# Experts' weights fetched in rows of 8 KB a partition instead of 4 KB

## The chip, the cores and the metric

One NeuronCore of a Trainium2 chip runs the kernel alone. The metric is device time in microseconds for one launch, and the kernel before took 886.41 us (median of 3 runs, 886.3 to 887.85). The engines are TensorE (PE, with its weight loads as PEld), VectorE (DVE), ScalarE (ACT), GpSimd (POOL) and SyncE (SP), which here only issues DMAs. Sixteen DMA engines move data between HBM and SBUF.

## The reference

The kernel computes one decoder layer for 512 tokens of width 1024 in float32: a combined projection, an HGRN2 branch and a stick-breaking attention branch, a mix with LayerNorm, a cross attention with LayerNorm, and a mixture of experts with a last LayerNorm. The change touches the weights of the last part:

```
for e in range(N_EXPERTS):                     # 16 experts, each token uses two of them
    hidden = jax.nn.silu(hf @ w1[e]) * (hf @ w3[e])    # w1[e], w3[e]: 1024 x 512
    y = y + combine[:, e:e + 1] * (hidden @ w2[e])     # w2[e]: 512 x 1024
```

Every expert reads 6.3 MB of weights, 2.1 MB for each matrix, and all sixteen are read whole.

## The kernel before

The program runs in the order of the layer. All weights come through one list: the class Weights keeps the sources in the order of use (`src`), a list of free buffers (`raw_free`), and issues one DMA from SP (line 54) as soon as a buffer comes free. A buffer holds 128 partitions x 4 KB, 512 KB in all. The dense part (everything up to the cross attention) splits each piece into two float32r parts on ACT and DVE (lines 65 and 67) and gives the buffer back at once. The experts' pieces are "plain": PE reads them as they land, and the buffer is given back by `done` when the expert is through. Towards the experts more and more SBUF becomes buffers (`ring`, `xres`, `s8`, `out` slots, parts of `sbk` and `wx`), until 44 of 512 KB are in use, three and a half experts' weights.

From expert 1 on a piece of w1 or w3 is two neighbouring rows of the matrix in each partition, 4 KB in a row; a piece of w2 is one row of 1024 numbers in each partition, 4 KB too. An expert has 12 pieces: four each of w1, w3 and w2. Expert 0 takes its rows 128 apart, 2 KB each.

The loop over the experts, in the order in which each engine meets it:

1. `up(e)`: PE multiplies the gathered tokens (64 columns) by w1 and w3 (line 1451); for more than 64 and 96 tokens two further parts follow under a branch (line 1462). ACT and DVE make the hidden values (lines 1472, 1473).
2. `turn_in(e + 1)`: eight transposes on PE (line 1424) of the next expert's tokens, which an indirect DMA of POOL has gathered (`gather`, line 1187). Then POOL issues the gather after that.
3. `down(e - 1)`: PE multiplies the hidden values of the expert before by its w2 (line 1492, further parts in line 1500) into `sums_down`.
4. `to_rows(e - 1)`: ACT (lines 1515, 1521) and then DVE (line 1523) scale the sums into the one tile `y_out`, and POOL adds its rows to the DRAM tensor `yd` by an indirect DMA (`scatter`, line 1301). `y_out` exists once, so `to_rows` of the next expert waits until this scatter has landed.
5. `turn_hidden(e)`: four transposes (line 1479), copied to SBUF on DVE (line 1481). DVE works in program order, so this copy stands behind `to_rows(e - 1)`, and `down(e)` needs it.

Steps 4, 5 and 3 make a ring: scatter lands, `to_rows` runs, the next scatter is issued, and so on; the copy behind `to_rows` holds the next `down` on PE. After the loop the last two experts are added without a scatter, and the last LayerNorm follows.

Of the kernel before, what the change touches and what calls it, by code (L numbers as in the profile page):

```python
# [24 lines left out]
class Weights:  # L25


    def __init__(self, nc, ahead):
        self.nc, self.ahead = nc, ahead
        self.other = ()  # L30
        self.src, self.raw_free, self.raw, self.parts = [], [], {}, {}
        self.out_free, self.own = [], {}
        self.kept = None
        self.plain = set()
        self.loaded = self.split = 0
        self.limit = 1 << 30

    def add(self, ap, plain=False):
# [5 lines left out]
        return j  # L44

    def buffers(self, raw=(), out=()):
        self.raw_free += raw
        self.out_free += out
        self.load()

    def load(self):
        while self.raw_free and self.loaded < len(self.src):
            ap, buf = self.src[self.loaded], self.raw_free.pop(0)
            self.nc.sync.dma_start(buf.rearrange("p (k n) -> p k n", n=ap.shape[-1]), ap)
            self.raw[self.loaded] = buf
            self.loaded += 1

    def prepare(self, upto):
        while self.split <= min(upto, self.limit, len(self.src) - 1):
            j = self.split  # L60
            if not self.out_free:
                return
            hi, lo = self.own[j] = self.out_free.pop(0)
            raw = self.raw.pop(j)
            self.nc.scalar.copy(hi, raw)  # L65
            eng = self.nc.gpsimd if j in self.other else self.nc.vector
            eng.tensor_tensor(lo, raw, hi.bitcast(F32), op=ALU.subtract)  # L67
            n = self.src[j].shape[-1]
            self.parts[j] = tuple(a.rearrange("p (k n) -> p k n", n=n) for a in (hi, lo))
            self.split += 1  # L70
            self.raw_free.append(raw)
            self.load()

    def get(self, j):
        if j in self.plain:
            return self.raw[j]
        self.prepare(j + self.ahead)
        return self.parts[j]

    def done(self, j):  # L80
        if j in self.plain:
            self.raw_free.append(self.raw.pop(j))
# [14 lines left out]
def tile_kernel(ctx, tc, x, mem, ln_in_g, ln_in_b, w_in, hg_lb_logits, hg_norm_g, w_branch_a, w_branch_b,  # L97
# [74 lines left out]
    outs = [out_tile(i) for i in range(4)]  # L172
    W.buffers([raws[:, i] for i in range(2)], outs)
    nc.sync.dma_start(xres[:, 1], x[P:2 * P])
    W.buffers([raws[:, i] for i in (2, 3)])
    for t in (2, 3):
# [270 lines left out]
    G = slot(10, [P, NT, 512], name="hgG")  # L447
    wx = pp.tile([P, 2, T], F32, name="wx")
    sbk = pp.tile([P, 2, T + 1], F32, name="sbk")
    oTa_h = oTa_l = None  # L450
# [261 lines left out]
    W.kept = None  # L712
    W.buffers([sbk.rearrange("p a n -> p (a n)")[:, 0:D]], [out_tile(3)])
    xres = pp.tile([P, NT, D], F32, tag="xres", name="xres1")
# [175 lines left out]
    def ring(tags):  # L890
        for i in tags:
            r = slot(i, [P, 2, D], name=f"ring{i}")
            rings[i] = [r[:, 0], r[:, 1]]
            W.buffers(rings[i])

# [79 lines left out]
    s8 = slot(8, [P, 2, D], name="s8")  # L975
    W.buffers([s8[:, 1], wx.rearrange("p a n -> p (a n)")])
    room = [s8[:, 0], rw.rearrange("p k n -> p (k n)")]
# [253 lines left out]
    more = take([10], I32, where=1)  # L1231

    natural_major([q_wo[1]], oc(0), oc(1), ev_wo, before=lambda t: begin(route_first(t), 2))
    for i in range(4):
        r = pp.tile([P, 2, D], F32, tag=f"out{i}", name=f"ringout{i}")
        W.buffers([r[:, 0], r[:, 1]])
    gather0(1, 0)
# [7 lines left out]
    route_fold(t)  # L1245
    W.buffers([xres[:, 0]])
    gather0(2, 0)
# [7 lines left out]
    gather0(3, 1)  # L1255
    s3 = slot(3, [P, 2, D], name="s3")
    W.buffers([s3[:, 1]])
    xgT = s3[:, 0].rearrange("p (k n) -> p k n", n=P)
# [3 lines left out]
    W.buffers([xres[:, 1]])  # L1262

# [126 lines left out]
    def tell():  # L1390
# [4 lines left out]
        yield 1  # L1395
        W.buffers([xres[:, 2], xres[:, 3]])
        count_blocks()
# [21 lines left out]
    def turn_in(e):  # L1419
        xg = gbr[:, 1].rearrange("t (q p k) -> t q k p", q=4, k=2)  # L1420
        for q in range(2):
            p = msp()
            for i in range(4):
                nc.tensor.transpose(p[:, i * P:(i + 1) * P], xg[:, 2 * q + i // 2, i % 2], ident)  # L1424
            (nc.scalar.copy, nc.vector.tensor_copy)[q](xgT[:, 4 * q:4 * q + 4],
# [17 lines left out]
    def up(e):  # L1443
        x, (a, b) = xgT, sums_up
        ws = []
        for q, js in enumerate(q_up[e]):
            ws.append([W.get(j) for j in js])
            for k in range(2):
                c = 2 * q + k
                for i, w in enumerate(reversed(ws[q])):  # L1450
                    nc.tensor.matmul(a[64 * i:64 * i + 64], x[:, c, 0:64], w[:, k * 512:(k + 1) * 512], start=c == 0,  # L1451
                                     stop=c == 7)
            tick()
        if e == 0:
# [3 lines left out]
        def part(g):  # L1458
            for c in range(8):
                for i in range(4):  # L1460
                    o = c % 2 * 512 + i % 2 * 256
                    nc.tensor.matmul(b[32 * i:32 * i + 32, 256 * g:256 * g + 256],  # L1462
                                     x[:, c, 64 + 32 * g:96 + 32 * g], ws[c // 2][i // 2][:, o:o + 256],
                                     start=c == 0, stop=c == 7)
# [10 lines left out]

    def turn_hidden(e, h, p=None):
        p = p or msp()
# [6 lines left out]
    def down(e):  # L1484

        x, (a, b) = hT.pop(e), sums_down
        ws = [W.get(j) for j in q_w2[e]]

        def base():
            for k, w in enumerate(ws):  # L1490
                for n in range(2):
                    nc.tensor.matmul(a[64 * n:64 * n + 64], x[:, k, 0:64], w[:, n * 512:(n + 1) * 512], start=k == 0,
                                     stop=k == 3)
                tick()

        def part(g):
            for k, w in enumerate(ws):
                s = slice(64 + 32 * (k // 2), 96 + 32 * (k // 2))
                for i in range(4):
                    nc.tensor.matmul(b[32 * i:32 * i + 32, 256 * g:256 * g + 256], x[:, 2 * g + k % 2, s],  # L1500
                                     w[:, 256 * i:256 * i + 256], start=k == 0, stop=k == 3)

# [23 lines left out]
    for e in range(NE - 1):  # L1526
# [4 lines left out]
        if e == 13:  # L1531
            scratch.extend(W.raw_free.pop() for i in range(4))
            more_blocks()
            W.buffers(scratch)
        if e == 0:
# [16 lines left out]
    def last_loads():  # L1552

        assert W.loaded == len(W.src)
        whole = [i for i in rings if all(any(b is f for f in W.raw_free) for b in rings[i])][:4]
        free.extend(b for b in W.raw_free if b is not s3[:, 1] and not any(b is h for i in whole for h in rings[i]))
        for t in (1, 2, 3, 0):
# [48 lines left out]
    yh[NE - 2], yl[NE - 2] = two_parts(rooms.pop(), "yg14")  # L1606
    yh[NE - 1], yl[NE - 1] = two_parts(3, "yg15")
    base, rest = down(NE - 2)
    base()

    p = msp()
    for i in range(4):
        nc.tensor.transpose(p[:, i * P:(i + 1) * P], h[:, i * P:(i + 1) * P], ident)
    x = work("w2k", [P, T], bufs=5).rearrange("p (k n) -> p k n", n=P)
# [5 lines left out]
    rest()  # L1620
    ws = [W.get(j) for j in q_w2[NE - 1]]
    for n in range(2):
        for k, w in enumerate(ws):
            nc.tensor.matmul(sums_up[n], x[:, k], w[:, halves[n]], start=k == 0, stop=k == 3)  # L1624
    for j in q_w2[NE - 1]:
# [95 lines left out]
```

## Time and profile before

| | us |
|---|---|
| median of 3 runs | 886.41 |
| profiled execution, its own time | 886.88 |
| span in the profile (first to last instruction) | 885.1 |
| PE busy | 847.2 (96%) |
| experts, from the first `up` to the last | 594.9 to 842 |

The page shows PE busy nearly throughout; the ends of matmuls are modelled there, so that a busy PE need not be one at its peak, and small gaps have to be looked for in the waits and the timeline. The DMA engines are nearly idle in the first two thirds and over 90% busy while the experts run, at some 350 to 390 GB/s.

### The profile page before, as it was taken

To read this page: it belongs to the slowest core of one execution; us is meant where nothing else is said; L and a number is where in the kernel's file an instruction comes from. 1 tells how busy PE (TensorE), PEld (TensorE's weight loads), DVE (VectorE), ACT (ScalarE), POOL (GpSimd) and SP (SyncE) were. 2 spreads that over 40 slices of the span, in tenths; PEclk is the share of its full clock that TensorE was granted. 3 is DMA by queue.
4 is the path that set the end of the run, shared out by engine and by line. 5 is a ranking of instruction groups with operands and counts; after the bars stand their busy time and mean duration, and the time that the engine had idled before them with its cause. 6 is when DMAs were issued, how large, how long until landed. Compare 5 with 4: busy or idle time off the path is not lost. (4 is left out here: it accounts for less than half of the span.)

```text
span 885.1 us, 13705 instructions
## 1 busy us (share of the span) xinstructions
PE 847.2 (96%) x5296; PEld 586.1 (66%) x5296; DVE 457.1 (52%) x806; ACT 337.7 (38%) x640; POOL 123.8 (14%) x212
## 2 busy tenths in 40 slices
PE   6999999999999999999999999997989999999994
PEld 5888777788777777888988888773333343344343
DVE  6632578644558554759744566684242322422336
ACT  2332336543554553422633444222332333323234
POOL 5400000000212220002200000221121111211102
PEclk8999999999999999999999999999999999999998
DMA  8443222222212227332742567599999999999952
GB/s 299 140 135 96 73 93 76 72 72 72 95 48 72 72 78 256 119 118 73 219 167 70 187 220 284 215 351 373 392 378 364 346 350 351 359 360 357 361 172 95
DMA packets 63908, 177.66 MB, mean 201 GB/s; under 512 B 7797, under 2 KB 7829, under 8 KB 63824
## 3 DMA queue, kind: packets, MB, share of 16 engines
q1 hardware_dynamic: 56144, 157.31, 49.6%
q0 software_dynamic: 7536, 18.65, 6.9%
q8 instruction: 60, 0.98, 0.4%
q10 hardware_dynamic: 144, 0.52, 0.1%
q14 instruction: 24, 0.20, 0.1%
HBM read 168.47 MB, written 15.73 MB: 208 GB/s over the span
## 5 line engine op out<-in xcount | busy, mean ns | idle before, releaser
L1523 DVE TENSOR_SCALAR ringgb<-I-5383_acc,wgb 32x256 f32<-32x256 f32 x60 | 29.2, 487 | 118.2 <-ACT ringgb L1521 116.7
L1451 PE MATMUL I-5377_acc<-ring,s 128*64 128x512 f32 x276 | 79.0, 596 | 0.0
L1515 ACT ACTIVATE ringgb<-I-5381_acc,wgb 64x512 f32<-64x512 f32 x30 | 20.5, 684 | 80.8 <-DMA yd<-ringgb,s 64.9
L67 DVE TENSOR_TENSOR I-69_out<-raws,I-69_out 128x1024 fp32r<-128x1024 f32 x24 | 29.4, 1224 | 38.3 <-ACT I-69_out L65 37.9
L1451 PEld LDWEIGHTS I-5377_acc<-ring,s 128*64 128x64 f32 x276 | 23.7, 137 | 34.0 <-issue 31.5
L1301 POOL DMA_INDIRECT yd<-ringgb,s x14 | 22.4, 1600 | 157.1 <-DVE I-8384w2k L1481 16.9
L663 DVE TENSOR_TENSOR_SCAN wx<-sbk 128x128 f32<-128x128 f32 (+3 forms) x32 | 27.1, 847 | 28.7 <-POOL sbk L659 28.7
L65 ACT CAST I-73_out<-raws 128x1024 fp32r<-128x1024 f32 x23 | 24.2, 1050 | 45.5 <-PE I-3558_acc L190 17.1
L67 DVE TENSOR_TENSOR I-71_out<-raws,I-71_out 128x1024 fp32r<-128x1024 f32 x23 | 28.1, 1224 | 24.6 <-ACT I-71_out L65 24.6
L65 ACT CAST I-69_out<-raws 128x1024 fp32r<-128x1024 f32 x25 | 26.3, 1050 | 32.7 <-issue 9.2
L67 DVE TENSOR_TENSOR I-73_out<-raws,I-73_out 128x1024 fp32r<-128x1024 f32 x22 | 26.9, 1223 | 16.1 <-ACT I-73_out L65 15.8
L65 ACT CAST I-71_out<-raws 128x1024 fp32r<-128x1024 f32 x24 | 25.3, 1054 | 24.9 <-PE I-384_acc L189 4.6
L1521 ACT ACTIVATE ringgb<-I-5383_acc,wgb 32x256 f32<-32x256 f32 x60 | 27.9, 464 | 4.3 <-issue 2.2
L1451 PE MATMUL I-5377_acc<-raws,s 128*64 128x512 f32 x60 | 27.8, 601 | 0.0
L659 POOL TENSOR_SCALAR_AFFINE_SELECT sbk<-sbk 128x128 f32<-128x128 f32 x32 | 14.3, 447 | 94.5 <-ACT sbk L654 50.2
L1462 PE MATMUL I-5379_acc<-ring,s 128*32 128x256 f32 x392 | 27.4, 380 | 0.0
L1451 PE MATMUL I-5377_acc<-ringout,s 128*64 128x512 f32 x92 | 25.0, 595 | 0.0
L1187 POOL DMA_INDIRECT ringgb<-x2d,s x15 | 15.7, 1045 | 49.3 <-PE I-5540_ms L1424 8.6
L1462 PEld LDWEIGHTS I-5379_acc<-ring,s 128*32 128x32 f32 x392 | 14.5, 110 | 12.1 <-issue 4.1
L216 POOL TENSOR_TENSOR I-1461hgss<-I-1461hgss,mhalf 128x4 f32<-128x4 f32 x1 | 1.0, 1047 | 136.9 <-DVE I-1461hgss L567 136.9
L966 POOL MEMSET I-4794w2k<- 128x128 f32 x1 | 0.2, 204 | 109.9 <-PE I-4740_ms L190 109.9
L1451 PEld LDWEIGHTS I-5377_acc<-ringout,s 128*64 128x64 f32 x92 | 7.6, 137 | 11.4 <-issue 11.1
(3506 smaller groups left out, 2410.3 us busy)
## 6 DMA issues: line engine op xcount, KB each, us to landing
ring<-in_moe_w_dram SPq DMA_DIRECT2D x107, 512.0 KB, 11.9
raws<-in_w_in_dram SPq DMA_DIRECT2D x44, 512.0 KB, 3.5
ringout<-in_moe_w_dram SPq DMA_DIRECT2D x32, 512.0 KB, 13.2
raws<-in_moe_w_dram SPq DMA_DIRECT2D x20, 512.0 KB, 11.2
xres<-in_moe_w_dram SPq DMA_DIRECT2D x16, 512.0 KB, 13.7
s<-in_moe_w_dram SPq DMA_DIRECT2D x8, 512.0 KB, 13.0
raws<-in_xa_wk_dram SPq DMA_DIRECT2D x7, 512.0 KB, 3.7
raws<-in_xa_wv_dram SPq DMA_DIRECT2D x7, 512.0 KB, 3.7
```

The lines of the kernel that those rows point to most:

```text
L65: self.nc.scalar.copy(hi, raw)
L67: eng.tensor_tensor(lo, raw, hi.bitcast(F32), op=ALU.subtract)
L216: nc.gpsimd.tensor_tensor(o, v, mhalf[:, :v.shape[-1]], op=ALU.pow)
L659: nc.gpsimd.affine_select(kp[:, d], kp[:, d], pattern=[[-1, P]], compare_op=ALU.is_gt, fill=1.0, base=w * (P - 1), channel_multiplier=1 - ...
L663: nc.vector.tensor_tensor_scan(rest[:, :n][:, ::-1], kp[:, n:0:-1], kp[:, n:0:-1], 1.0, ALU.mult, ALU.bypass)
L1187: nc.gpsimd.indirect_dma_start(out=gbr[:, 1], out_offset=None, in_=x2d[:, :], in_offset=bass.IndirectOffsetOnAxis(ap=gidx[:, e:e + 1], axi ...
L1301: nc.gpsimd.indirect_dma_start(out=yd[:, :], out_offset=bass.IndirectOffsetOnAxis(ap=idx, axis=0), in_=y, in_offset=None, bounds_check=T - ...
L1451: nc.tensor.matmul(a[64 * i:64 * i + 64], x[:, c, 0:64], w[:, k * 512:(k + 1) * 512], start=c == 0, stop=c == 7)
L1462: nc.tensor.matmul(b[32 * i:32 * i + 32, 256 * g:256 * g + 256], x[:, c, 64 + 32 * g:96 + 32 * g], ws[c // 2][i // 2][:, o:o + 256], start ...
L1515: nc.scalar.activation(y[0:64, n * 512:(n + 1) * 512], a[s], AF.Copy, scale=gates_at[s, 0, e:e + 1])
L1521: nc.scalar.activation(o, z, AF.Copy, scale=f)
L1523: nc.vector.tensor_scalar(o, z, f, None, op0=ALU.mult)
```

## The change

A piece of the experts' weights becomes twice as large, and so does the row that a partition gets: four neighbouring rows of w1 and w3 (4 x 2 KB), two of w2 (2 x 4 KB), 8 KB in a row, 1 MB a piece. An expert has six pieces instead of twelve. Expert 0 takes four blocks of 2 KB a partition, in pieces of 1 MB too. The buffers become 8 KB wide, 22 of them; `halve`, `free` and `room` split one in two for the dense part's 4 KB pieces and join it again when both halves are free. `wx` and `sbk` become one tile, and `xgT` moves from slot 3 to half of `s8`, so that slot 3 is a whole wide buffer.

Since the rows of a matrix lie otherwise over the partitions, the tokens and the hidden values are turned to match: `turn_in` takes every fourth column instead of every second, and `turn_hidden` every second instead of neighbouring ones. The matmuls keep their number, shapes and order.

```
-        while self.raw_free and self.loaded < len(self.src):
-            ap, buf = self.src[self.loaded], self.raw_free.pop(0)
-            self.nc.sync.dma_start(buf.rearrange("p (k n) -> p k n", n=ap.shape[-1]), ap)
+        while self.loaded < len(self.src):
+            ap = self.src[self.loaded]
+            k, n = ap.shape[1:]
+            buf = self.room(k * n == 2048)
+            if buf is None:
+                return
+            self.nc.sync.dma_start(buf.rearrange("p (k n) -> p k n", n=n), ap)
...
+    def free(self, buf):
+        wide, other = self.pair.get(id(buf), (None, None))
+        if wide is not None and self.is_free(other):
+            self.raw_free = [b for b in self.raw_free if b is not other] + [wide]
+        else:
+            self.raw_free.append(buf)
...
-            q_up[e] = [tuple(W.add(w[0, e, 2 * q * P:(2 * q + 2) * P].rearrange("(k p) n -> p k n", p=P) if e == 0 else
-                                   w[0, e, 2 * q * P:(2 * q + 2) * P].rearrange("(p k) n -> p (k n)", k=2)[:, None], True)
-                             for w in (moe_w1, moe_w3)) for q in range(4)]
+            q_up[e] = [tuple(W.add(w[0, e, 4 * q * P:(4 * q + 4) * P].rearrange("(k p) n -> p k n", p=P) if e == 0 else
+                                   w[0, e, 4 * q * P:(4 * q + 4) * P].rearrange("(p k) n -> p (k n)", k=4)[:, None], True)
+                             for w in (moe_w1, moe_w3)) for q in range(2)]
         if e > 0:
-            q_w2[e - 1] = [W.add(moe_w2[0, e - 1, k * P:(k + 1) * P].rearrange("(k p) n -> p k n", p=P), True)
-                           for k in range(4)]
+            q_w2[e - 1] = [W.add(moe_w2[0, e - 1, 2 * q * P:(2 * q + 2) * P].rearrange("(p k) n -> p (k n)", k=2)[:, None],
+                                 True) for q in range(2)]
...
-        xg = gbr[:, 1].rearrange("t (q p k) -> t q k p", q=4, k=2)
+        xg = gbr[:, 1].rearrange("t (q p k) -> t q k p", q=2, k=4)
...
+    def turned_hidden(h):
+        p = msp()
+        hq = h.rearrange("t (q p k) -> t q k p", q=2, k=2)
         for i in range(4):
-            nc.tensor.transpose(p[:, i * P:(i + 1) * P], h[:, i * P:(i + 1) * P], ident)
+            nc.tensor.transpose(p[:, i * P:(i + 1) * P], hq[:, i // 2, i % 2], ident)
```

On SP the refill of the buffers in the middle of the experts reads as follows before (each row a DMA of 4 KB a partition; L1438 is a branch of the experts' further parts):

```order
L54 DMA ring9_4584<-in_moe_w3_dram 128x1024
L54 DMA ring9_4584<-in_moe_w1_dram 128x1024
L54 DMA ring10_4587<-in_moe_w3_dram 128x1024
L54 DMA ring10_4587<-in_moe_w1_dram 128x1024
L54 DMA raws_68<-in_moe_w3_dram 128x1024
L54 DMA ring13_4609<-in_moe_w1_dram 128x1024
L1438 UNCONDITIONAL_BRANCH
L54 DMA ring13_4609<-in_moe_w3_dram 128x1024
```

And with the change, at the like place:

```order
L91 DMA raws_68<-in_moe_w3_dram 128x2048
L91 DMA ring13_4602<-in_moe_w1_dram 128x2048
L91 DMA ring11_4700<-in_moe_w3_dram 128x2048
L1479 UNCONDITIONAL_BRANCH
L91 DMA ring12_4702<-in_moe_w2_dram 128x2048
```

A slot is filled by one DMA of 128x2048 where it took two of 128x1024; w1 and w3 still alternate. On PE `up` of one expert reads before, in its second half (each buffer serves two steps, and w3 and w1 lie in halves of the same slots):

```order
L1451 MATMUL I-5377_acc_5378<-ringout2_5243,s3_5346 64x512
L1451 MATMUL I-5377_acc_5378<-ringout1_5240,s3_5346 64x512
L1451 MATMUL I-5377_acc_5378<-ringout2_5243,s3_5346 64x512
L1451 MATMUL I-5377_acc_5378<-ringout1_5240,s3_5346 64x512
L1451 MATMUL I-5377_acc_5378<-ringout3_5246,s3_5346 64x512
```

And with the change:

```order
L1493 MATMUL I-5355_acc_5356<-ring11_4700,s8_4884 64x512
L1493 MATMUL I-5355_acc_5356<-ring13_4602,s8_4884 64x512
L1493 MATMUL I-5355_acc_5356<-ring11_4700,s8_4884 64x512
L1493 MATMUL I-5355_acc_5356<-ring13_4602,s8_4884 64x512
L1493 MATMUL I-5355_acc_5356<-ring6_4704,s8_4884 64x512
```

The matmuls are the same; a slot now holds one matrix, serves four steps, and its first matmul waits for a DMA of 1 MB. ACT, DVE and POOL keep every instruction of the loop in its place.

## Rows read from the trace of the kernel before

**Rows 1.** The page: busy us, share of the span and instructions of each engine, and GB/s of the DMA engines in 40 slices of 22.1 us.

```profile
PE 847.2 (96%) x5296; PEld 586.1 (66%) x5296; DVE 457.1 (52%) x806; ACT 337.7 (38%) x640; POOL 123.8 (14%) x212
GB/s 299 140 135 96 73 93 76 72 72 72 95 48 72 72 78 256 119 118 73 219 167 70 187 220 284 215 351 373 392 378 364 346 350 351 359 360 357 361 172 95
```

**Rows 2.** The waits of PE and of its weight loads from 590 to 860 us (two answers): who waited for whom, us in total, times, longest.

```profile
PE I-5533_ms L1424 <- DMA ringgb<-x2d,s: 4.3, 1, 4.3
PE I-5381_acc L1492 <- issue: 2.2, 1, 2.2
...
PEld I-5377_acc L1451 <- DMA ring<-in_moe_w_dram: 1.7, 6, 0.3
PEld I-5381_acc L1492 <- DMA ringout<-in_moe_w_dram: 1.4, 3, 0.6
```

**Rows 3.** The instructions of single lines: what ACT's line 1515 (the start of `to_rows`) waited for (us, times), then the landing of the scatter (line 1301), then the landing of the gather (line 1187).

```profile
  DMA yd<-ringgb,s: 64.9, 10
...
DMA to landing us min/median/max: 8.2/9.0/9.9
...
DMA to landing us min/median/max: 7.2/8.1/10.3
```

**Rows 4.** The timeline of one lap, 700 to 722 us, from ACT, DVE and POOL: start, length, engine and line, in brackets the idle time before and what ended it.

```profile
700.35 1.39 ACT L1515 ACTIVATE ringgb<-I-5381_acc,wgb 64x512 f32<-64x512 f32 x2 [4.11 <-DMA yd<-ringgb,s]
...
703.74 2.05 DVE L1523 TENSOR_SCALAR ringgb<-I-5383_acc,wgb 32x256 f32<-32x256 f32 x4 [6.96 <-ACT ringgb L1521]
705.82 0.69 DVE L1481 COPY I-6744w2k<-I-6738_ms 128x512 f32<-128x512 f32 x1
...
706.56 1.60 POOL L1301 DMA_INDIRECT yd<-ringgb,s  x1 [9.18 <-DVE I-6744w2k L1481]
...
715.73 1.39 ACT L1515 ACTIVATE ringgb<-I-5381_acc,wgb 64x512 f32<-64x512 f32 x2 [4.24 <-DMA yd<-ringgb,s]
```

**Rows 5.** The timeline at five places, DVE's copy (line 1481) and the `down` on PE that needs it (line 1492), and at one place the start of `to_rows` and the scatter before it.

```profile
644.70 0.69 DVE L1481 COPY I-5984w2k<-I-5978_ms 128x512 f32<-128x512 f32 x1
...
645.65 1.08 PE L1492 MATMUL I-5381_acc<-s,I-5984w2k 128*64 128x512 f32 x4
...
659.97 0.69 DVE L1481 COPY I-6174w2k<-I-6168_ms 128x512 f32<-128x512 f32 x1
...
660.76 1.36 PE L1492 MATMUL I-5381_acc<-ring,I-6174w2k 128*64 128x512 f32 x4 [2.15 <-issue]
...
721.93 1.60 POOL L1301 DMA_INDIRECT yd<-ringgb,s  x1 [9.48 <-DVE I-6934w2k L1481]
...
733.74 1.40 ACT L1515 ACTIVATE ringgb<-I-5381_acc,wgb 64x512 f32<-64x512 f32 x2 [3.48 <-PEq L1438]
...
739.20 0.69 DVE L1481 COPY I-7124w2k<-I-7118_ms 128x512 f32<-128x512 f32 x1
...
742.88 3.65 PE L1492 MATMUL I-5381_acc<-ring,I-7124w2k 128*64 128x512 f32 x16
...
770.56 0.69 DVE L1481 COPY I-7504w2k<-I-7498_ms 128x512 f32<-128x512 f32 x1
...
771.36 1.22 PE L1492 MATMUL I-5381_acc<-raws,I-7504w2k 128*64 128x512 f32 x3 [0.38 <-ACT s L1425]
...
772.78 2.79 PE L1492 MATMUL I-5381_acc<-ring,I-7504w2k 128*64 128x512 f32 x11
...
786.60 0.69 DVE L1481 COPY I-7694w2k<-I-7688_ms 128x512 f32<-128x512 f32 x1
...
791.50 1.94 PE L1492 MATMUL I-5381_acc<-ring,I-7694w2k 128*64 128x512 f32 x8
```

**Rows 6.** DMA queues in three stretches: packets, MB, share of 16 engines' time. First 338 to 341 us (q0 is POOL's queue with rows of 4 KB, q1 is SP's with rows of 2 KB), then 727 to 729 us (q0 holds a scatter, q1 the experts' weights in rows of 4 KB), then q0 from 721.9 to 731.2 us, from the issue of that scatter to its landing.

```profile
q0 software_dynamic: 196, 0.79, 64.2%
q1 hardware_dynamic: 208, 0.42, 38.1%
...
q1 hardware_dynamic: 138, 0.52, 66.5%
q0 software_dynamic: 41, 0.14, 33.9%
...
q0 software_dynamic: 144, 0.27, 14.8%
```

**Rows 7.** One stretch by engine (busy us and instructions of PE, PEld, DVE, ACT and POOL, then the granted clock, DMA share and GB/s), and the last row of the `down` that began at 660.76 us.

```profile
662.00:664.00 2.00, 2.00 (x8) 0.75 (x6) 0.78 (x2) 0.00 (x0) 1.36 (x2) 0.50 0.90 344
...
663.55 2.56 PE L1492 MATMUL I-5381_acc<-ring,I-6174w2k 128*64 128x512 f32 x8
```

**Rows 8.** The transposes: weight loads of `turn_in` (every second column) and `turn_hidden` (neighbouring columns), ns min, median, max; then the eight of one `turn_in` on the timeline.

```profile
L1424 PEld LDWEIGHTS I-5683_ms<-ident,ringgb x4: 209/209/209, 617.9 to 618.2; 128*128 128x128 f32 x4
...
L1479 PEld LDWEIGHTS I-5788_ms<-ident,I-5670w2k x4: 137/142/143, 623.6 to 623.9; 128*128 128x128 f32 x4
...
709.93 0.71 PE L1424 MATMUL I-6852_ms<-ident,ringgb 128*128 128x128 f32 x4 [0.31 <-PEq L1438]
710.49 0.64 PE L1424 MATMUL I-6859_ms<-ident,ringgb 128*128 128x128 f32 x4
```

**Rows 9.** The last weights on SP's timeline, and the start of `up(15)` on PE's.

```profile
827.13 8.57 SPq L54 DMA_DIRECT2D ring<-in_moe_w_dram  x6
...
835.64 0.64 PE L1451 MATMUL I-5377_acc<-raws,s 128*64 128x512 f32 x1
```

More of the change, by code (lines that the diff above doesn't have):

```diff
@@ L172, in tile_kernel @@
     outs = [out_tile(i) for i in range(4)]
-    W.buffers([raws[:, i] for i in range(2)], outs)
+    raw2 = [raws[:, i:i + 2].rearrange("p a n -> p (a n)") for i in (0, 2)]
+    W.buffers([raw2[0]], outs)
     nc.sync.dma_start(xres[:, 1], x[P:2 * P])
-    W.buffers([raws[:, i] for i in (2, 3)])
+    W.buffers([raw2[1]])
     for t in (2, 3):
@@ L891, in ring @@
         for i in tags:
-            r = slot(i, [P, 2, D], name=f"ring{i}")
-            rings[i] = [r[:, 0], r[:, 1]]
-            W.buffers(rings[i])
+            rings[i] = slot(i, [P, 2 * D], name=f"ring{i}")
+            W.buffers([rings[i]])
     rings, attended = {}, []
@@ L1255, in tile_kernel @@
     gather0(3, 1)
-    s3 = slot(3, [P, 2, D], name="s3")
-    W.buffers([s3[:, 1]])
-    xgT = s3[:, 0].rearrange("p (k n) -> p k n", n=P)
+    rings[3] = slot(3, [P, 2 * D], name="ring3")
+    W.buffers([rings[3]])
+    xgT = s8[:, 1].rearrange("p (k n) -> p k n", n=P)
     for q in range(2):
@@ L1444, in up, with w @@
         x, (a, b) = xgT, sums_up
[L1445 to L1453, printed above, removed]
+        def w(i, c, o, n):
+            return W.cut(q_up[e][c // 4][i], c % 4 * 512 + o, n)
+        for c in range(8):
+            for i in range(2):
+                nc.tensor.matmul(a[64 * i:64 * i + 64], x[:, c, 0:64], w(1 - i, c, 0, 512), start=c == 0, stop=c == 7)
+            if c % 2:
+                tick()
         if e == 0:
@@ L1486, in down, with w @@
         x, (a, b) = hT.pop(e), sums_down
-        ws = [W.get(j) for j in q_w2[e]]
+        def w(k, o, n):
+            return W.cut(q_w2[e][k // 2], k % 2 * D + o, n)
         def base():
-            for k, w in enumerate(ws):
+            for k in range(4):
                 for n in range(2):
-                    nc.tensor.matmul(a[64 * n:64 * n + 64], x[:, k, 0:64], w[:, n * 512:(n + 1) * 512], start=k == 0,
-                                     stop=k == 3)
+                    nc.tensor.matmul(a[64 * n:64 * n + 64], x[:, k, 0:64], w(k, n * 512, 512), start=k == 0, stop=k == 3)
                 tick()
         def part(g):
-            for k, w in enumerate(ws):
+            for k in range(4):
                 s = slice(64 + 32 * (k // 2), 96 + 32 * (k // 2))
@@ L1531, in tile_kernel @@
         if e == 13:
-            scratch.extend(W.raw_free.pop() for i in range(4))
+            lent = [b for b in W.raw_free if b.shape[-1] == 2048][-2:]
+            W.raw_free = [b for b in W.raw_free if not any(b is i for i in lent)]
+            scratch.extend(h for b in lent for h in W.halve(b))
             more_blocks()
-            W.buffers(scratch)
+            W.buffers(lent)
         if e == 0:
@@ L1554, in last_loads @@
         assert W.loaded == len(W.src)
-        whole = [i for i in rings if all(any(b is f for f in W.raw_free) for b in rings[i])][:4]
-        free.extend(b for b in W.raw_free if b is not s3[:, 1] and not any(b is h for i in whole for h in rings[i]))
+        whole = [i for i in rings if W.is_free(rings[i])][:5]
+        for b in W.raw_free:
+            if not any(b is rings[i] for i in whole):
+                free.extend(W.halve(b) if b.shape[-1] == 2048 else [b])
+        free.append(s8[:, 1])
         for t in (1, 2, 3, 0):
@@ L1620, in tile_kernel @@
     rest()
-    ws = [W.get(j) for j in q_w2[NE - 1]]
     for n in range(2):
-        for k, w in enumerate(ws):
-            nc.tensor.matmul(sums_up[n], x[:, k], w[:, halves[n]], start=k == 0, stop=k == 3)
+        for k in range(4):
+            nc.tensor.matmul(sums_up[n], x[:, k], W.cut(q_w2[NE - 1][k // 2], k % 2 * D + n * T, T), start=k == 0, stop=k == 3)
     for j in q_w2[NE - 1]:
```

68 lines of the change are left out of this document (44 added, 24 removed).

## Prediction

> **What bounds the kernel now.** I read the page first: PE is busy 847 us, 96% of the span, and the DMA engines move some 350 to 390 GB/s only in the last third, where the experts run [rows 1]. So the first question is whether PE waits for weights there. The list of waits says no: in 270 us the longest single wait for a weight DMA is 0.6 us, and the two groups shown come to 3.1 us together [rows 2]. The waits that count are others: 4.3 us for the first gathered tokens, and one of 2.2 us before a `down` [rows 2].
>
> The rows of `to_rows` tell what the second one is. Its start waited ten times (of fourteen possible) for the scatter before it to land, 64.9 us in all; a scatter takes 9.0 us from issue to landing [rows 3]. One lap of this ring can be read off the timeline [rows 4]: ACT from 700.35, DVE 703.74 to 705.79, scatter issued at 706.56, landed before ACT starts again at 715.73. That is 6.2 us of work and 9.2 us of DMA, 15.4 us a lap, whatever PE does. PE's own pace depends on the tokens: between the `down`s at 645.65 and 660.76 lie 15.1 us of which 2.15 were idle [rows 5], so a light expert costs PE 12.96 us, less than a lap; heavy experts cost it more. PE and the ring therefore take turns. At 645.65 PE starts 0.26 us after the copy it needs (644.70 + 0.69), at 660.76 it has waited 2.15 us, at 742.88 it has 2.99 us to spare, at 771.36 it has waited 0.38 us, at 791.50 it has 4.21 us to spare [rows 5]. Both are co-critical up to 771 us, and PE alone after it.
>
> **The change, part by part.** *The weight stream.* How a row's length acts on its DMA is shown at 338 to 341 us, where two queues ran side by side [rows 6]. Rows of 4 KB: 0.642 x 16 engines x 3 us / 196 = 157 ns each. Rows of 2 KB: 0.381 x 48 us / 208 = 88 ns. The second 2 KB cost 69 ns, so a row of 8 KB should take 157 + 2 x 69 = 295 ns instead of 2 x 157 = 314. A megabyte is 8 rows on each of 16 engines, 2.36 us instead of 2.51, so the stream is relieved by 6%. To the path this is worth nothing, because PE does not wait for the stream [rows 2]. The last `up` begins at 835.64 while the last weights are issued from 827.13 to 835.70 [rows 9]; earlier weights are spare there, too. The cover of this zero is the 44 buffers; if PE became several us faster, the weights would be late at the end.
>
> *The gathers and scatters that share the engines.* The same two rows show how two queues share: 196 packets against 208, one for one, though one kind is twice as long [rows 6]. The engine takes turns by packet and not by bytes. From 727 to 729 us a scatter shares with the weights: 0.14 MB are 34 rows of 4 KB, 0.339 x 32 us / 34 = 319 ns each; with one weight row of 157 ns after each, 34 x 476 ns = 16.2 us of engine time in 2 us, that is 8 of the 16 engines. From issue to landing the scatter moves 0.27 MB, 66 rows of 4 KB [rows 6], so 8 rows an engine and 8 turns of 476 ns, 3.8 us of its 9.0 (spread over all 16 engines it would be 4 turns).
>
> The Trainium skill says the same of the turns, but not of the unit: "DMA: Bandwidth & Descriptors", section "Queues, rings and completion order", lets each engine go round its queues packet by packet, with typically 9 to 17 descriptors to a packet. The trace's one-to-one count agrees with the turns and speaks against so large a packet. By that rule a scatter's rows would go in one or two turns and the landing would hardly grow.
>
> With rows of 8 KB each turn costs 295 instead of 157 ns, 138 more. Eight turns and the row that is under way when the first one arrives make 9 x 0.138 = 1.24 us more for each scatter and each gather. No row shows a packet of 8 KB in this queue, so the bounds: below, nothing or -0.2 us (if the engine shares by bytes, or a row is cut at 4 KB; and 6% less stream in the 3.6 us of the landing that are neither POOL's 1.60 us nor the 3.8 us of turns); above, +4.4 us (if these 3.6 us also were weight rows ahead of the scatter, 3.6 x 138 / 157 = 3.2). I take 1.24, since the rows at 338 us are the nearest.
>
> *What of it reaches the path.* (a) The gather that PE waits for at 607 us: +1.24, directly [rows 2]. (b) The `down` at 771.36 is expert 10's; its copy stands behind `to_rows(9)`, which waits for scatter 8, so nine landings (scatters 0 to 8) lie ahead of it, and each adds 1.24: 11.2 us. That `down` had no slack. But at 733.74 the ring waited for PE (its idle time ended at PE's branch), 2.8 us after the scatter issued at 721.93 would have landed (721.93 + 9.0 = 730.9) [rows 3, 5]; that slack is used up first: 11.2 - 2.8 = 8.4. What PE has to spare between (2.99 at 742.88) changes nothing, since the later zero counts. After 771 PE has 4.2 us to spare and gains on the ring, so two or three later landings cost nothing. (c) The clock. The `down` after the 2.15 us gap took 5.35 us (660.76 to 663.55 + 2.56), where the one at 742.88 took 3.65; the granted clock was 0.50 from 662 to 664 us, 1.2 of 2.4 GHz [rows 5, 7]. The gap at 771 us grows from 0.38 to some 5 us; that `down` took 4.21 us before (771.36 to 772.78 + 2.79 [rows 5]) and should take 5.35 now: +1.1.
>
> *The rest.* The transposes read their columns further apart. Doubling the step once raised a weight load from 142 to 209 ns [rows 8], and yet eight of them took 1.20 us at 709.93 (709.93 to 710.49 + 0.64; 150 ns each), less than the 209 of one load [rows 8]; the load is hidden behind the matmul before. `turn_hidden` now has that step: nothing. For `turn_in` the step doubles again: nothing to 8 x 138 ns = 1.1 us an expert; I take nothing, by the nearest row. PE's first matmul of a slot waits for 1 MB instead of 512 KB, hidden by the buffers that are three experts ahead. In the dense part the 4 KB pieces take the same halves in the same order; POOL, ACT and DVE keep their order. I count nothing.
>
> Sum: 1.24 + 8.4 + 1.1 = 10.7 us. On the profiled execution's 886.88 us (1.8 us more than its span) this is 897.6; the median of the runs lay 0.47 us lower, so 897.1 us.
>
> **The rivals.** *Turns do not lengthen* (by bytes, or a row cut in two at 4 KB): nothing changes on the path, 886.4 us. For it: no row shows an 8 KB packet of SP. Against it: 196 to 208 [rows 6].
>
> The Trainium skill bears on this one: the same page's section "SWDGE vs HWDGE vs iDMA" calls a packet preferably at most 4096 B. If that is a limit for the hardware queue, this rival holds; the trace has no packet of SP above 4 KB.
>
> *The stream's relief reaches the ring* (the other side, faster): with 6% less stream and half as many pieces, gathers and scatters start sooner. The price: at most the waits that are PE's now, 2.2 and 0.4 us, the slow clock behind the first, 1.7, and a little of the 4.3: some 4.4 us, 882.5 us if all of it goes, 884 if half. It decides from the point where a landing falls below 9.0 - 2.15 / 3 us, so that three laps give back the gap at 660 us. For it: the 3.6 us in a landing that the turns do not explain. Against it: the stream stays dense from 600 to 845 us either way.
>
> The same page's "Measured" table sides with the change: it asks for 1 MB a DMA (estimate: its 341 GB/s against 138 at 64 KB). The waits [rows 2] say that PE would not be reached.
>
> *`turn_in` pays for its step*: up to 1.1 us an expert; in the laps it hides behind the ring, in the five experts after 771 us it does not: +4 to +5, 902 us. For it: 142 to 209 ns. Against it: hidden so far.
>
> *More weight rows stand ahead of a scatter* than one: each further one adds 0.138 us a lap, seven of them 1 us, nine laps 9 us: 906 us.
>
> **How the numbers follow.** Turns longer by about 1.2 us, with or without the third and fourth rival, 0.76: slower. No longer turns, 0.14: the same. The relief, 0.10: faster. What this kernel's measurement can tell from no change is 0.2%, 1.8 us. The forecast is 897 us, with 892 to 909 if the turns lengthen. The range of 8 in 10 reaches down to 885, through the middle of the unchanged case, and up to 909, where a scatter has seven more rows ahead of it.
>
> **What would show it.** The scatter's landing should have a median of 10.2 us and the gather's of 9.3; ACT's line 1515 should wait for scatters about 12 times; the weights' queue should hold packets of 8 KB that take 290 to 320 ns; PE should be idle some 5 us before the `down` that was at 771 us and 3 to 4 before the one at 661; the last weights should land earlier against the `up` that reads them. If the scatter still lands after 9.0 us, the step on the turns is wrong; if it lands later and the time has not grown, the walk through the laps is.

## The result and the profile after

The kernel after takes 897.24 us (median of 6 runs, 895.69 to 898.93) beside 887.76 us for the kernel before on the same chip (6 runs, 886.3 to 889.15). The ratio is 1.011, with a 95% interval from 1.0097 to 1.0123: 8.6 to 10.9 us slower. The profiled execution took 898.93 us, 1.7 us more than its span, and so stands at the upper end of its runs, as that of before (886.88) stands at the lower end of its own. Between the two profiles lie 12.1 us; the medians are 9.5 us apart.

The page after: busy times of the engines, GB/s in 40 slices (of 22.4 us), and the weights' queue (packets, MB, share of 16 engines).

```profile
PE 850.9 (95%) x5296; PEld 588.8 (66%) x5296; DVE 457.0 (51%) x806; ACT 337.9 (38%) x640; POOL 123.9 (14%) x212
...
GB/s 304 154 108 94 95 72 95 71 47 95 71 70 71 71 163 168 141 69 158 217 100 59 200 316 177 300 414 340 401 403 390 384 364 363 370 362 321 70 156 94
...
q1 hardware_dynamic: 42832, 157.30, 47.6%
```

The same instructions run and PE is busy 3.7 us longer, though no operation on it was added [rows 1]; most of that is slow clock behind PE's waits, as will be seen. The queue moves its 157.30 MB in 42832 packets instead of 56144. By the trace's records of single packets, 11776 of them have 8192 bytes, and the median one takes 309 ns (159 ns for 4096 bytes in the kernel before). A row of 8 KB thus stands in the trace as one packet.

Next, the waits after: PE's, then ACT's at the start of `to_rows` (now line 1562; who waited for whom, us in total, times, longest).

```profile
PE I-5506_ms L1465 <- DMA ringgb<-x2d,s: 5.9, 1, 5.9
PE I-7521_ms L1465 <- DMA ringgb<-x2d,s: 4.1, 1, 4.1
...
PE I-5359_acc L1540 <- issue: 2.7, 2, 1.4
...
PE I-6233_ms L1465 <- DMA ringgb<-x2d,s: 2.2, 1, 2.2
...
ACT ringgb L1562 <- DMA yd<-ringgb,s: 100.3, 12, 12.0
```

ACT waits for scatters 12 times and 100.3 us [rows 3: 10 and 64.9]. PE has two waits that were not there before: 2.2 and 4.1 us for gathered tokens, at `turn_in` (line 1465), each shortly before a `down` [rows 2]. The landings, by line: the scatter (1342), then the gather (1228), min, median and max.

```profile
DMA to landing us min/median/max: 5.8/10.2/11.2
...
DMA to landing us min/median/max: 7.8/10.9/13.6
```

The scatter's median grew by 1.2 us, the gather's by 2.8 [rows 3]. How they work together shows in the timeline of the lap that costs most (start, length, engine and line, idle time before and what ended it):

```profile
764.04 1.60 POOL L1342 DMA_INDIRECT yd<-ringgb,s  x1 [14.45 <-DVE I-7233w2k L1527]
...
765.95 1.04 POOL L1228 DMA_INDIRECT ringgb<-x2d,s  x1 [0.31 <-issue]
...
775.04 1.39 ACT L1562 ACTIVATE ringgb<-I-5359_acc,wgb 64x512 f32<-64x512 f32 x2 [12.01 <-DMA yd<-ringgb,s]
778.43 2.04 DVE L1570 TENSOR_SCALAR ringgb<-I-5361_acc,wgb 32x256 f32<-32x256 f32 x4 [12.28 <-ACT ringgb L1568]
779.68 1.10 PE L1465 MATMUL I-7521_ms<-ident,ringgb 128*128 128x128 f32 x4 [4.05 <-DMA ringgb<-x2d,s]
780.50 0.69 DVE L1527 COPY I-7417w2k<-I-7411_ms 128x512 f32<-128x512 f32 x1
...
781.57 3.68 PE L1540 MATMUL I-5359_acc<-ring,I-7417w2k 128*64 128x512 f32 x8
```

Scatter 8 is issued at 764.04 and releases ACT at 775.04. Its `to_rows` ends on DVE at 780.47, and only then does DVE copy the hidden values that `down(10)` needs (780.50 to 781.19). The gather stands on POOL behind that same scatter: it goes out at 765.95, as soon as POOL is free and before the scatter has moved its rows, and it lands 13.6 us later. PE, done with `up(11)` at 775.6, waits for it until 779.68 and begins `down(10)` at 781.57, 0.4 us after the copy was ready. So two chains that start from one scatter end together, and PE's wait is put down to the gather alone, since that ended first in program order.

The issue times of the scatters show the ring's lateness lap by lap (from the two timelines):

| scatter | 0 | 1 | 2 | 3 | 4 | 5 | 6 | 7 | 8 | 9 |
|---|---|---|---|---|---|---|---|---|---|---|
| before | 629.79 | 645.44 | 660.71 | 675.83 | 691.03 | 706.56 | 721.93 | 739.94 | 755.10 | 771.30 |
| after | 629.93 | 647.13 | 663.38 | 679.81 | 696.18 | 713.67 | 730.14 | 746.64 | 764.04 | 781.24 |
| later by | 0.14 | 1.69 | 2.67 | 3.98 | 5.15 | 7.11 | 8.21 | 6.70 | 8.94 | 9.94 |

A lap costs 1.35 us more on average up to scatter 6. At scatter 7 the lateness falls by 1.5: there the ring of before had waited for PE. Behind it two laps cost 2.24 and 1.00 us more.

Last, the clock (PE's busy time and the others', then granted clock, DMA share, GB/s) behind the wait at 780 us:

```profile
780.00:782.00 2.00, 2.00 (x10) 1.53 (x10) 1.91 (x4) 0.59 (x1) 0.76 (x1) 0.50 1.07 324
782.00:784.00 2.00, 2.00 (x6) 0.47 (x4) 1.32 (x2) 0.00 (x0) 1.70 (x2) 0.50 0.88 373
```

It is at the lower level, 1.2 GHz, after PE had been idle for 4.05 us. That `down` lasts 5.41 us [rows 5: 4.21], the one at 663.43 us 6.45 us [rows 5 and 7: 5.35].

### The profile page after: what moved, and what is told of

It reads as the page before. It is cut to its first block, busy times and chain, and to the rows that moved or that the text cites. A ratio compares the mean times of both kernels' runs of the same rounds, so it can differ in the third digit from the quotient of the medians.

```text
span 897.2 us, 13529 instructions
## 1 busy us (share of the span) xinstructions
PE 850.9 (95%) x5296; PEld 588.8 (66%) x5296; DVE 457.0 (51%) x806; ACT 337.9 (38%) x640; POOL 123.9 (14%) x212
## 3 DMA queue, kind: packets, MB, share of 16 engines
q1 hardware_dynamic: 42832, 157.30, 47.6%
## 5 line engine op out<-in xcount | busy, mean ns | idle before, releaser
L1570 DVE TENSOR_SCALAR ringgb<-I-5361_acc,wgb 32x256 f32<-32x256 f32 x60 | 29.2, 487 | 142.1 <-ACT ringgb L1568 140.6
L1493 PE MATMUL I-5355_acc<-ring,s 128*64 128x512 f32 x312 | 97.1, 601 | 0.0
L1562 ACT ACTIVATE ringgb<-I-5359_acc,wgb 64x512 f32<-64x512 f32 x30 | 20.5, 683 | 108.7 <-DMA yd<-ringgb,s 100.3
L1493 PEld LDWEIGHTS I-5355_acc<-ring,s 128*64 128x64 f32 x312 | 29.2, 138 | 39.8 <-issue 38.2
L1342 POOL DMA_INDIRECT yd<-ringgb,s x14 | 22.4, 1600 | 179.3 <-DVE I-8287w2k L1527 17.0
L705 DVE TENSOR_TENSOR_SCAN wsb<-wsb 128x128 f32<-128x128 f32 (+3 forms) x32 | 27.1, 847 | 28.7 <-POOL wsb L701 28.7
L1503 PE MATMUL I-5357_acc<-ring,s 128*32 128x256 f32 x416 | 30.7, 380 | 0.0
L1568 ACT ACTIVATE ringgb<-I-5361_acc,wgb 32x256 f32<-32x256 f32 x60 | 27.9, 464 | 3.8 <-issue 1.7
L1493 PE MATMUL I-5355_acc<-raws,s 128*64 128x512 f32 x64 | 28.7, 596 | 0.0
L1493 PE MATMUL I-5355_acc<-ringout,s 128*64 128x512 f32 x88 | 28.5, 596 | 0.0
L1503 PEld LDWEIGHTS I-5357_acc<-ring,s 128*32 128x32 f32 x416 | 16.2, 110 | 12.8 <-issue 4.1
L1493 PEld LDWEIGHTS I-5355_acc<-ringout,s 128*64 128x64 f32 x88 | 8.6, 137 | 10.1 <-issue 9.7
```

The costliest lines, as they stand in the source:

```text
L705: nc.vector.tensor_tensor_scan(rest[:, :n][:, ::-1], kp[:, n:0:-1], kp[:, n:0:-1], 1.0, ALU.mult, ALU.bypass)
L1342: nc.gpsimd.indirect_dma_start(out=yd[:, :], out_offset=bass.IndirectOffsetOnAxis(ap=idx, axis=0), in_=y, in_offset=None, bounds_check=T - ...
L1493: nc.tensor.matmul(a[64 * i:64 * i + 64], x[:, c, 0:64], w(1 - i, c, 0, 512), start=c == 0, stop=c == 7)
L1562: nc.scalar.activation(y[0:64, n * 512:(n + 1) * 512], a[s], AF.Copy, scale=gates_at[s, 0, e:e + 1])
L1568: nc.scalar.activation(o, z, AF.Copy, scale=f)
L1570: nc.vector.tensor_scalar(o, z, f, None, op0=ALU.mult)
```

## The experiments

The theory: an engine takes turns between its queues row by row, so a weight row of 8 KB makes every gather and scatter row wait longer, and the ring of `to_rows` and scatter carries this to PE. The rivals: it is the 1 MB piece or its buffer; the strides of the transposes; the gather alone; the sum of bytes and engine time. The ratios are to the kernel before on the same chip; runs 1 to 4, 5 to 8, and 9 and 10 shared a chip each. Not every DMA's landing is recorded in their traces (10 of 14 scatters in runs 1 and 4), so their medians are of those that are.

**1. Rows of 4 KB in pieces of 1 MB.** The kernel after with

```
-  w[0, e, 4*q*P:(4*q+4)*P].rearrange("(p k) n -> p (k n)", k=4)[:, None]
+  w[0, e, 4*q*P:(4*q+4)*P].rearrange("(a p k) n -> p a (k n)", a=2, k=2)
-  moe_w2[0, e-1, 2*q*P:(2*q+2)*P].rearrange("(p k) n -> p (k n)", k=2)[:, None]
+  moe_w2[0, e-1, 2*q*P:(2*q+2)*P].rearrange("(k p) n -> p k n", p=P)
```

and the transposes of before.

> The kernel after with its 1 MB pieces, its 8 KB buffers and its order kept, but each piece laid out as two rows of 4 KB on a partition (transposes read as in the kernel before). Theory (a turn of an engine lasts as long as a row, so scatters and gathers that share the engines land later): packets of 4 KB at about 159 ns again, scatter landing 9.0 us and gather landing 8.1 us in the median, PE's wait for the gather before the `down` at 782 us gone, time 885 to 888.5 us. Rival (the size of a piece, of its buffer or the wait for 1 MB costs the time, not the row): landings as in the kernel after, 10.2 and 10.9 us, time about 897 us.

Measured: 888.94 us, ratio 1.0019 (1.0005 to 1.0033). Landings of scatter and gather, by line:

```profile
DMA to landing us min/median/max: 9.1/9.4/10.7
...
DMA to landing us min/median/max: 7.4/8.2/10.8
```

PE's waits:

```profile
PE I-5359_acc L1540 <- issue: 4.5, 2, 2.3
PE I-5506_ms L1465 <- DMA ringgb<-x2d,s: 4.5, 1, 4.5
...
PE I-7521_ms L1465 <- DMA ringgb<-x2d,s: 0.9, 1, 0.9
```

The row's length is the cause: pieces, buffers and order are those of the kernel after, and some 8 of its 9.5 us are gone. What is left, 0.2%, is just above what can be told from nothing. The landing, though, is 9.4 us and not the 9.0 expected. The packet records tell why. Take the start of a scatter's ninth row of 4 KB, and the stretch from there to the landing (medians of the first twelve scatters, as far as recorded): 5.1 and 4.2 us before, 5.2 and 5.1 in the kernel after, 5.3 and 4.0 here. So the stretch of the rows, which is what the theory is about, follows the row's length alone; what run 1 has more than the kernel before lies ahead of the rows. The wait at `turn_in` was to go and is 0.9 us; the `down` behind it begins after a further wait of 2.25 us and lasts 6.74 us here.

**2 and 9. One matrix at a time in rows of 8 KB.** Run 2 keeps the long rows for w2 alone, run 9 for w1 and w3 alone (the other edit of run 1 is undone).

> As the run with rows of 4 KB, but w2 (a third of the bytes) in rows of 8 KB as in the kernel after. Theory: a third of the long turns, so a scatter lands 0.4 us later than in the kernel before (9.4 us) and a gather that follows one 0.9 us later; time 888 to 891.5 us. Rival (pieces, not rows): 897 us. If the loss came all from w1 and w3's wider stride in the transposes: as the run with 4 KB rows.

> w1 and w3 (two thirds of the bytes, half of the rows) in rows of 8 KB, w2's 1 MB pieces in rows of 4 KB, transposes accordingly. With w2 alone in rows of 8 KB a fifth of the rows was long, and yet two thirds of the loss came. If each scatter pays for the mean of the rows that it meets: half of 1.2 us a scatter, 9 of them 5 us, 892 to 894 us, and then w2's share in that run is unexplained. If the slowest of the engines decides and a single long piece in the way is enough: scatters at 10.0 to 10.3 us in the median and 894 to 897.5 us, nearly the whole loss again.

Measured: w2 alone 894.69 us, ratio 1.0083 (1.0061 to 1.0105); w1 and w3 alone 893.84 us, ratio 1.0078 (1.005 to 1.0106). The scatter's landing with w2 alone:

```profile
DMA to landing us min/median/max: 9.0/10.2/11.1
```

and with w1 and w3 alone:

```profile
DMA to landing us min/median/max: 6.0/10.1/11.0
```

With w2 alone the expectation was missed: the scatter lands as late as with all rows long (10.2 against the 9.4 expected), and the time is 3 us above the range. In run 9 the landing came out as the slowest engine would have it, the time as the mean of the rows would. The two losses, about 7 and 6 us, each hold run 1's 1.6 us; beyond it they come to some 10 us where both together cost 8, which the intervals do not tell apart. The landings do not add up either: they are 0.8 and 0.7 us above run 1's, and 0.8 with all rows long. That would fit landings that are set by the slowest engine, where one long piece in the way is enough. But run 2's own trace speaks against that, and against the mean as well. Two of its scatters, issued at 646.78 and 709.38 us, each from its first row to its landing (651.6 to 655.8 and 714.3 to 719.8 us):

```profile
DMA packets 434, 1.55 MB, mean 368 GB/s; under 512 B 162, under 2 KB 162, under 8 KB 329
```

```profile
DMA packets 599, 1.98 MB, mean 361 GB/s; under 512 B 167, under 2 KB 167, under 8 KB 549
```

Beside the first, 105 of the 272 packets of at least 2 KB have 8 KB or more, and it lands after 9.0 us, as with no long row. Beside the second it is 50 of 432, and it lands after 10.4. Neither the share of long rows nor the mere presence of some sets the landing here, and the trace does not say which engine a row ran on. Why w2 alone does most of the harm stays open.

**3. The strides alone.** Run 1 with the transposes of the kernel after.

```
-  xg = gbr[:, 1].rearrange("t (q p k) -> t q k p", q=4, k=2)
+  xg = gbr[:, 1].rearrange("t (q p k) -> t q k p", q=2, k=4)
-  ... h[:, i * P:(i + 1) * P] ...
+  ... hq[:, i // 2, i % 2] ...
```

> As the run with rows of 4 KB, but with the transposes of the kernel after (every fourth column for the tokens, every second for the hidden values); the rows then meet the wrong columns, so the output is another, the work is the same. Theory: the strides cost PE 0.1 us an expert at most (turn_hidden's four take 0.71 us in the kernel after, 0.62 before), so the same time as the run with 4 KB rows within 1.5 us. Rival (strided transposes pay): up to 1.1 us an expert for the tokens, in the five experts after 771 us and the light ones before, 4 to 9 us more than that run.

Measured: 888.84 us, ratio 1.0011 (0.9998 to 1.0023), 0.1 us from run 1. The four transposes of `turn_hidden` at the same place of run 3 and of run 1:

```profile
717.78 0.75 PE L1521 MATMUL I-6859_ms<-ident,I-6779w2k 128*128 128x128 f32 x4 [0.46 <-PEq L1481]
```

```profile
713.86 0.66 PE L1521 MATMUL I-6859_ms<-ident,I-6779w2k 128*128 128x128 f32 x4 [0.46 <-PEq L1481]
```

That is 0.09 us an expert, and nothing for `turn_in`, whose second four take 0.64 us in both. The rival falls.

**4. Shorter rows.** The kernel before with w1 and w3 in rows of 2 KB.

```
-  w[0, e, 2*q*P:(2*q+2)*P].rearrange("(p k) n -> p (k n)", k=2)[:, None]
+  w[0, e, 2*q*P:(2*q+2)*P].rearrange("(k p) n -> p k n", p=P)
```

> The kernel before with w1 and w3 in rows of 2 KB (two on a partition a piece; transposes read neighbouring columns), w2 in rows of 4 KB as before. Theory (turns): two thirds of the weight rows last 84 to 88 instead of 157 ns, so a scatter lands 9 x 0.07 x 2/3 = 0.4 us sooner (8.6 us) and a gather behind one 0.9 us sooner; PE's waits of 2.2 us at 660 us and 0.4 us at 771 us shrink or go and with them the slow clock behind the first: 883 to 886 us. Against that the stream is some 5% slower, and the last weights have little to spare: if PE then waits for weights near the end, up to 892 us. Rival (only the sum of bytes and time on the engines counts): scatters land later than in the kernel before, time 888 to 895 us.

Measured: 895.65 us, ratio 1.0096 (1.0076 to 1.0116). The scatter's landing:

```profile
DMA to landing us min/median/max: 8.5/8.7/10.2
```

What ACT waited for from 840 to 870 us, and the weights' queue (packets, MB, share of 16 engines) from 840 to 844 us:

```profile
ACT zp L193 <- DMA ring<-yd: 6.2, 2, 5.8
```

```profile
q1 hardware_dynamic: 404, 1.45, 91.7%
```

The ring did as the theory says (8.7 us for 9.0; the stretch of the rows is 3.6 us for 4.2), and `down(10)` began at 766.40 us, 5 us sooner than in the kernel before, though 1.6 of them were there already at scatter 0 (628.17 for 629.79). The time was missed, and it is near the rival's, whose later landings did not come. The stream is too slow: from 840 to 844 us the weights still hold 91.7% of the engines, where in the kernel before they hold 25.4%. SP waits at a branch (L1295) for the last weights: in the kernel before the last three land at 842.90, 844.16 and 846.58 us, and SP passes its waits there some 0.02 us after each; in run 4 it passes the same three at 849.39, 850.64 and 851.90. So its first read of `yd`, which in the kernel before follows the last scatter's landing at once (847.81 and 847.96 us), is issued at 852.46. ACT stands 5.8 us before its split of that tile, and the copies behind it hold PE's last matmuls for 5.0 us. Before that, PE waits 2.9 us inside `down(10)` and the clock falls. Shorter turns are bought with a slower stream, and the stream has nothing to spare.

**5. Gathers one expert sooner.** Both rows of xres that were lent to the weights are kept back; one is a second buffer for tokens.

```
-    W.buffers([W.halve(xrow[0])[0]])
-    W.buffers([W.halve(xrow[0])[1]])
+    x_in = [xres[:, 0], gbr[:, 1]]
-        if e + 2 < NE: gather(e + 2)
+        if e + 3 < NE: gather(e + 3)
```

> The kernel after with two buffers for gathered tokens (the second is a row of xres that is no longer lent to the weights, and its neighbour is kept back as well), so that each gather is issued one expert sooner; scatters and their one buffer stay. Theory (the ring of to_rows and scatter carries the loss, the gather only stood in front of the same `down`): PE's waits of 2.2 and 4.1 us for gathered tokens go, but the `down`s at 663 and 782 us start as late, up to 1 us sooner, since their copies wait for the scatters: 893 to 897.5 us. Rival (the gather behind a scatter carries the loss): PE gets to those `down`s 2 and 4 us sooner and the slow clock goes with it: 887 to 891 us.

Measured: 896.29 us, ratio 1.0094 (1.0065 to 1.0123). Waits of PE, then of ACT:

```profile
PE I-5358_acc L1540 <- issue: 7.4, 2, 4.1
```

```profile
ACT ringgb L1562 <- DMA yd<-ringgb,s: 98.9, 12, 11.8
```

The waits of 2.2 and 4.1 us for gathers are gone, and the same time is now lost one step later, before the `down`: 4.13 us idle at 775.51. The gather alone carried nothing that the ring did not.

**6. Two buffers for `to_rows`.** Again both rows are kept back; one is a second `y_out`.

```
-    y_out = gbr[:, 0]
+    y_out = [gbr[:, 0], xres[:, 1]]
-        y = y_out
+        y = y_out[e % 2]
```

> The kernel after with two buffers for to_rows (a row of xres; its neighbour is kept back as well), so that to_rows waits for the scatter before the last; gathers stay as they are. Theory (ring): ACT's 12 waits of 100 us for scatters go, the `down`s wait for no copy; the gathers that follow a scatter still take 11 to 13 us and hold some turn_in for up to 1 us: 885 to 890 us. Rival (gather): the waits of 2.2 and 4.1 us at turn_in stay, 892 to 896 us.

Measured: 888.58 us, ratio 1.0006 (0.9991 to 1.002). Waits of ACT over the run, of PE from 760 to 790 us, and the stretch behind them with its clock:

```profile
ACT ringgb L1560 <- PE I-5358_acc L1538: 26.0, 7, 4.6
```

```profile
PE I-5354_acc L1491 <- DMA ring<-in_moe_w_dram: 3.8, 2, 2.9
```

```profile
782.00:784.00 2.00, 2.00 (x8) 0.61 (x4) 0.00 (x0) 0.00 (x0) 0.00 (x0) 0.55 0.97 348
```

With rows of 8 KB in place, a second buffer gives the whole loss back. In `to_rows` ACT now waits for PE and no longer for a scatter. `down(10)` begins at 766.26 us, 15.3 us sooner than in the kernel after. Then PE meets the next limit: at `up(12)` it waits 3.8 us for weights, the clock falls, and that `up` lasts 11.9 us instead of 7.1.

**7 and 8. Both second buffers, with rows of 8 KB (7) and of 4 KB (8).**

> Both second buffers. Theory: no landing of a scatter or of a later gather is left on PE's path, so PE alone sets the pace of the experts; the kernel before had 2.2 + 0.4 us of idle PE and about 2.2 us of slow clock behind them, the kernel after begins the experts 2.1 us sooner and pays 1.6 us more for the first gather: 880 to 884 us, if two buffers fewer do not make the weights late. Rival (something else in rows of 8 KB, such as the stream or the transposes, holds PE): 888 us or more.

> Both second buffers with the 1 MB pieces in rows of 4 KB. Theory: where no landing is on the path, a row's length is worth nothing, so within 2 us of the run with rows of 8 KB and both buffers, sooner by 1 to 1.5 us at most for the first gather: 879 to 884 us. Rival (rows of 8 KB cost PE elsewhere): sooner than that run by 4 us or more.

Measured: 887.9 us, ratio 0.9999 (0.9981 to 1.0017), and 888.46 us, ratio 1.0005 (0.9993 to 1.0017). Where no landing of a scatter is on the path, the row's length makes no difference that can be measured. The level was missed by 4 us: both wait for weights, run 7 for 3.9 us at `up(12)` and run 8 for 2.3 us at `up(11)`, the condition that the expectation of run 7 named. Run 8 stands 1.4 us more inside `down(10)` and 2.6 us before `up(12)`, which the list of waits does not put down to weights. These kernels have two buffers of 4 KB fewer for the weights, and no run tells how much of the waiting comes from that.

**10. Two buffers for `to_rows` in the kernel before** (one row of xres kept back; the edit of run 6).

> The kernel before (pieces and rows of 4 KB) with a second buffer for to_rows; the weights have 43 buffers for 44. It gives the price of the ring in the kernel before. Theory (the ring cost it 2.2 + 0.4 us of idle PE and some 2 us of slow clock up to 771 us, but in the runs without the ring PE then caught up with the weights at 772 to 785 us): PE reaches expert 10's `down` 4 to 6 us sooner and waits for weights in the next two `up`s, so 884 to 889 us. Rival (the ring is all that holds the experts back): 880 to 883 us.

Measured: 887.46 us, ratio 0.9992 (0.9981 to 1.0003). PE's waits from 590 to 850 us:

```profile
PE I-5532_ms L1423 <- DMA ringgb<-x2d,s: 3.3, 1, 3.3
PE I-5376_acc L1450 <- DMA ring<-in_moe_w_dram: 2.0, 3, 0.7
PE I-5380_acc L1491 <- issue: 1.6, 1, 1.6
```

The kernel before gains nothing that can be measured: PE reaches `up(12)` 4.8 us sooner (771.46 for 776.28; 2.1 of them were there already at scatter 0, 627.65 for 629.79), waits there for weights and is 2.2 us sooner at `up(13)`; at the last matmuls, which wait 2.1 us for copies on ACT, 0.7 us are left. So at that point the ring and the stream seem about equally late in the kernel before; with one buffer fewer for the weights, run 10 cannot show it exactly. No run beats the kernel before by more than can be measured.

## Why the prediction was right

**The weight stream.** Right in kind, too large in size: a row of 8 KB takes 309 ns and not 295, beside 2 x 159 ns, so the relief is 3% and not 6%. That it is worth nothing on the path was right. The cover of this zero was named as the 44 buffers, with weights late at the end if PE became several us faster. Runs 6 to 8 and 10, with one or two buffers fewer, show them late already between 759 and 780 us.

**Turns by row.** Right, for the scatter and for rows of one length: +1.24 us forecast, +1.2 in the median, and by the table 1.35 us a lap. Run 1 shows that the length of the row makes it, and the rival that the turns do not lengthen falls. That it comes about turn by turn, one weight row for each small row, is the reading that fits uniform rows (runs 1 and 4); the mixed rows of runs 2 and 9 do not follow it. The Trainium skill ("DMA: Bandwidth & Descriptors", section "SWDGE vs HWDGE vs iDMA") calls a packet preferably at most 4096 B. The trace does not agree for SP's queue: it has rows of 8192 bytes as single packets.

**The gather** was mis-sized: 1.24 us more was forecast, 2.8 us were measured. Gathers that go out alone grew as forecast (8.6 and 8.4 us at 803 and 821 us, 7.2 and 7.3 at 792 and 809 us before). Those that POOL issues 0.3 us behind a scatter take 11.7 to 13.6 us, where such took 9.4 to 10.3, and there are six of them instead of three, because the later ring brings scatter and gather together more often. That their rows wait for the scatter's rows as well, and so pay for both sets of turns, fits these numbers; it is not shown row by row. The step counted each of them by itself.

**(a) The first gather:** +1.24 forecast; PE's wait grew by 1.6 (5.9 for 4.3), the landing itself by 1.0 (8.4 us for 7.4). The other 0.6 come from the start: in the profile after the experts began 2.1 us sooner (592.81 for 594.93), while this gather was issued only 1.55 us sooner. That is no effect of the change: runs 1 and 3 have the same dense part and begin at 592.00 and 595.08. The step left out that the `up` behind the longer wait is slower too, 7.94 us for 7.24 (granted clock 0.73 for 0.94 from 610 to 612 us).

**(b) Nine landings minus 2.8 us of slack:** 8.4 forecast for the ring, and scatter 9 is 9.8 us later than scatter 0 would make it (9.94 - 0.14). The slack was what the step said: 1.35 us more and 1.5 us less lateness make 2.85 us used up at scatter 7. The rest is the larger laps, above all the one from scatter 7 to 8 (2.24 us more). `down(10)` begins 10.2 us later, 1.24 + 8.4 = 9.6 were forecast. Only the look of it was other than foreseen: the wait appears at `turn_in`, for the gather. Runs 5 and 6 show that the ring carries it: a gather issued sooner gives back 1 us by the medians, within their intervals, and a second `y_out` 9.

**(c) The clock:** +1.1 forecast for `down(10)`, +1.2 measured. The `down` at 663 us is slower by 1.1 as well, but from there to 771 us the ring sets the pace and not PE, so it counts for nothing.

**The rest.** `turn_in`'s stride costs nothing, as taken, and the rival of 4 to 5 us falls; `turn_hidden` pays 0.09 us an expert where nothing was counted. After `down(10)` the distance grows by 0.6 us more, from 11.5 at `up(12)` to 12.1 at the last matmuls, of which the four later `turn_hidden` make some 0.4. The rival with more weight rows ahead of a scatter falls: its ninth row starts 5.2 us after the issue where it was 5.1, and the growth lies behind that. (The prediction's upper end of 909 us is put where seven more rows stand ahead; its own working gives 906 for them.) The relief that reaches the ring is refuted: all landings of scatters grew but the last, which met no weights any more (5.8 us for 8.2).

The sum of 10.7 us lies inside the measured 8.6 to 10.9, and part of that closeness is luck. In the two profiles the terms come to some 14 us: 2.3 for (a) with the slower `up`, 9.8 for the ring, 1.2 for the clock and 0.7 for the rest. The earlier start takes 2.1 off, which leaves the 12.1 between the profiles, and these stand 1.7 us above and 0.9 under the medians of their kernels. So the path, the waits and the direction are confirmed; the single terms were sized too small by about 3 us in this pair of executions.

## What to carry to other kernels

A longer row of a large transfer can make every small transfer on the same engines land later: before rows are made longer, look for gathers and scatters that stand in a ring with compute, and count the landings in it. If a wait ends at one DMA, look at what its issue was queued behind. Here a second buffer in the ring took the price of the long rows away (run 6), and where rows were short it gained nothing (run 10), because the next limit, the weights, was close.

## What was not expected of the hardware

Long rows in w2 alone, or in w1 and w3 alone, delay a scatter nearly as much in the median as in all three (10.2 and 10.1 us against 10.2, with 9.4 for none), so the cost does not follow the share of long rows. The last scatter of the kernel after, which meets no weights, lands after 5.8 us: its ninth row starts 2.2 us after the issue instead of 5.2. That 3 us is more than any row length changed, and the rows' length hardly moves it (5.1 to 5.3 us in the kernels before and after and in runs 1 to 4 and 9); what holds the first rows back stays open. And a gap in PE's work costs more than its length: behind the 4.05 us of the kernel after the granted clock is 0.50 and the next `down` takes 5.41 us for 4.21, and the `up` of run 6 that holds 2.9 us of waiting takes 11.9 us for 7.1, that is 1.9 us more than the wait.
